# One of two pairs of weight sums taken ahead, during the up projection, and two more steps of the down projection by seven products

## The chip, the cores and the metric

The kernel runs on one core of a Trainium2 chip. The metric is the device time of one execution in microseconds; lower is better. The median before is 1215.54 us of 3 runs (1215.43 to 1217.35).

## The reference

The kernel computes one layer of a hybrid decoder for 256 tokens (and 16 prepended ones, dropped from the output) of width 2048, all in float32. What matters here is the last part, the gated feed-forward network:

```python
u = rmsnorm(h, norm_ffn)
up = causal_dwconv(u @ w_up, ffn_conv_w, ffn_conv_b)     # 2048 -> 2 x 5632
gate, val = jnp.split(up, [FFN_DIM], axis=-1)
h = h + (jax.nn.silu(gate) * val) @ w_down               # 5632 -> 2048
h = rmsnorm(h, norm_final)                               # then 16 tokens dropped
```

Ahead of it come the input projection, eight retention heads, four mLSTM heads and the output projection. They aren't touched.

## The kernel before, in words

**Products.** TensorE multiplies in a reduced format (`F32R`), so every operand is split: ScalarE casts it to a high part, VectorE subtracts to get the low part, and a product takes three matmuls (high by high, high by low, low by high). `load_w` (L122) does this for weights: an SP load into `wraw` (4 buffers), the cast into `whi` (5 buffers, L128) and the subtraction into `wlo` (5 buffers, L130).

**Up projection.** The 44 column blocks of the feed-forward width are done in two halves of 22 (`NHF`). For each, `project` (L147) runs twice, for gate and value, each over two half tiles of 512 KB: 48 matmuls with the weights stationary and 258 columns of `uh` and `ul` moving (L137 to L140). The result is scaled out of PSUM by VectorE (L626), passed through the convolution (`conv3`), the gate's SiLU and the product, and split for the down projection: into `mh`, `ml` where the step is a plain one, into `sh`, `sl` where it goes by seven products. For the latter GpSimd (POOL) also makes four sums of blocks (L735 to L738) in `x_tile(0)`. During the first half VectorE transposes `h` from `hT` into `hn` (L622), four blocks at a time from j = 2 to 17; after that `hT` holds nothing that is needed.

**Down projection.** After each half of the up projection its 22 blocks are multiplied by their rows of `w_down`: 11 steps (`NQD`), each of two blocks, for two pairs of output column blocks (b = 0 and b = 2; each block has 512 columns). A plain step takes 2 x 512 KB through `load_step`, and `product` (L747) makes four products of 6 matmuls of 512 columns, 24 in all, into the four banks `cs`. A fast step (`FAST`, six of eleven) is a 2 x 2 block product by Winograd's form with seven block products of 3 matmuls, 21 in all (`seven`, L765). Its weights come in one 1 MB load into one of two places in the dead `hT` (`left`, two turns, L773). VectorE then makes four sums of weight blocks: two at once in `ta` (L776), and one each in `tb` (L777, L778); ScalarE and VectorE split four groups of blocks (L707, L709) and TensorE multiplies (L792 to L795), partly into `cs`, partly into four banks `ps` that are shared between blocks. After the last fast step `share` (L813) combines `ps` into the residual stream `hn` by DMAs that accumulate (`onto`, L811, POOL's queue).

**The last pass** (half 1, b = 2) runs its steps in an order written out by hand, with step `BOTH` done plainly from the fast step's splits, and leaves the second column block of the last `lag` = 4 plain steps for the end (`alone`): first for row block 0, whose norm and output then run (`gather`, `finish`) while TensorE does row block 1 in two pieces of 256 columns. Ahead of that, squares and gains of finished blocks (`squares` on ScalarE, `times_gain` on POOL) are hung behind fast steps; `reached` (L801) is a one-column POOL read that sets their place.

**Order.** Each engine works through its own queue in order. The queues are ordered by the compiler's scheduler, which simulates when each instruction could start and may place work well ahead of its place in the program (the first `hT<-in_wd` load is issued at 683.83 us, some 40 us ahead of its use); `tc.issue_after` pins single instructions.

Of the kernel before, what the change touches and what calls it, by code (L numbers as in the profile page):

```python
# [10 lines left out]
F32 = mybir.dt.float32  # L11
F32R = mybir.dt.float32r
# [4 lines left out]
P = 128  # L17
# [66 lines left out]
def trunk(ctx: ExitStack, tc: tile.TileContext, io, out: bass.AP):  # L84
# [18 lines left out]
        a = _COLS[name][0]  # L103
        return par[:, a + i : a + i + n]

    ident = consts.tile([P, P], F32, name="ident")
    ones = consts.tile([P, P], F32, name="ones")
    nc.vector.memset(ones, 1.0)
    inv_dm = consts.tile([P, P], F32, name="inv_dm")
    nc.vector.memset(inv_dm, 1.0 / DM)  # L110
    inv_ret = consts.tile([P, P], F32R, name="inv_ret")
    inv_ml = consts.tile([P, P], F32R, name="inv_ml")
    epsc = consts.tile([P, 1], F32, name="epsc")
    nc.vector.memset(epsc, EPS)
    rstd1 = consts.tile([P, T], F32, name="rstd1")
    rstd2 = consts.tile([P, NQ], F32, name="rstd2")
    norms = consts.tile([P, RH + 2 * MH], F32, name="norms")


    last_load = None  # L120
# [54 lines left out]

    pa_cm = pool("pa", 1, side="right")
    pa = pa_cm.__enter__()
    xh = pa.tile([P, KT, T], F32R, name="xh")
    xl = pa.tile([P, KT, T], F32R, name="xl")
    rope = pa.tile([P, 4, T], F32, name="rope")  # L180
# [388 lines left out]
    wk2_cm = pool("wk2", 2, side="right")  # L569
    wk2 = wk2_cm.__enter__()  # L570

    ssq = up.tile([P, NQ], F32, name="ssq")
    sq2_cm = pool("sq2", 2, side="right")
    sq2 = sq2_cm.__enter__()

# [28 lines left out]
    def norm2():  # L604
        ms2 = at.tile([P, 512], F32, name="atps")
        nc.tensor.matmul(ms2[:, :NQ], inv_dm, ssq, start=True, stop=True)
        r0, rt = (midp.tile([P, 512], F32, name=f"x{i}") for i in range(2))
# [5 lines left out]
    midp = midp_cm.__enter__()  # L613
    NHF = NF // 2
    ss4 = midp.tile([P, 2, 5], F32, name="ss4")

    def transposed_h(i, a):

# [77 lines left out]
    def x_tile(i):  # L696
        return midp.tile([P, 512], F32, name=f"x{i}")

    for half in range(2):
        mh = midp.tile([P, 2 * len(PLAIN), SEQ], F32R, name="mh")  # L700
        ml = midp.tile([P, 2 * len(PLAIN), SEQ], F32R, name="ml")
        sh = midp.tile([P, len(FAST), 7, P], F32R, name="sh")
# [8 lines left out]
        for jj in range(NHF):  # L711
            j = half * NHF + jj
            pair = []
            for s in range(2):
                pair.append(project(io["wu"][2 * j + s], uh, ul, 0))
                if j == 0 and s == 0:
                    norm2()
            gt = conv3(pair[0], j, "gt")
            vt = conv3(pair[1], NF + j, "vt")
            nc.scalar.activation(gt, gt, AF.Silu)  # L720
            nc.vector.tensor_tensor(out=gt, in0=gt, in1=vt, op=ALU.mult)
            q, i = divmod(jj, 2)
            if q in PLAIN:
                k = 2 * PLAIN.index(q) + i
                copied, parted = split(mh[:, k, :], ml[:, k, :], gt)
            elif i == 0:
                f = FAST.index(q)
                even = gt
                copied, parted = split(sh[:, f, A11, :], sl[:, f, A11, :], gt[:, 0:P])
            else:  # L730
                e11, e21, e12, e22 = even[:, 0:P], even[:, P:], gt[:, 0:P], gt[:, P:]
                if half == 1 and q == BOTH:
                    split(*a21, e21)
                sums = x_tile(0).rearrange("p (a t) -> p a t", a=4)
                nc.gpsimd.tensor_tensor(out=sums[:, S1, :], in0=e21, in1=e22, op=ALU.add)  # L735
                nc.gpsimd.tensor_tensor(out=sums[:, S3, :], in0=e11, in1=e21, op=ALU.subtract)
# [28 lines left out]
        def seven(b, q, cs, ps, first, last, after, norm):  # L765
# [7 lines left out]
            nc.sync.dma_start(raw, io["wd7"][b // 2, half * NQD + q])  # L773
            ta, tb = (wpool.tile([P, 2, 512], F32, name="wraw", bufs=4) for _ in range(2))

            nc.vector.tensor_tensor(out=ta, in0=raw[:, 1:3, :], in1=raw[:, 0:1, :].to_broadcast([P, 2, 512]), op=ALU.subtract)  # L776
            nc.vector.tensor_tensor(out=tb[:, 0, :], in0=raw[:, 2, :], in1=ta[:, 0, :], op=ALU.add)  # L777
            nc.vector.tensor_tensor(out=tb[:, 1, :], in0=raw[:, 3, :], in1=tb[:, 0, :], op=ALU.subtract)  # L778
            copied = None
            for w, to in (  # L780
                (raw[:, 2:4, :], ((S4, cs[0, 1], False, False), (A12, cs[0, 0], False, False))),
                (raw[:, 1:2, :], ((A11, ps[0], first, last),)),
                (ta, ((S1, ps[3], first, last), (S3, ps[1], first, last))),
                (tb, ((S2, ps[2], first, last), (A22, cs[1, 0], False, False))),
            ):
                hi = wpool.tile([P, 2, 512], F32R, name="whi", bufs=5)
                lo = wpool.tile([P, 2, 512], F32R, name="wlo", bufs=5)
# [8 lines left out]
            if norm:  # L796

                with tc.issue_after(copied.ins):
                    for g in norm:
                        squares(*g)  # L800
                reached = nc.gpsimd.tensor_tensor(out=junk[:, 0:1], in0=tb[:, 1, 0:1], in1=tb[:, 1, 0:1], op=ALU.add)  # L801
# [8 lines left out]

            nc.gpsimd.dma_start(block(tt, b), x, accum_op=ALU.add)  # L811

        def share(ps, b):  # L813

            p1, p7, p6, p5 = ps
            x6, x7, x5, x1 = (x_tile(i) for i in range(4))
# [7 lines left out]
            nc.vector.tensor_tensor(out=x5, in0=x7, in1=p5, op=ALU.subtract)  # L824
            onto(1, b + 1, x5)

# [13 lines left out]
        def load_step(b, q, to=wpool):  # L840
            return load_w(io["wd"][b, half * NQD + q], [P, 2, 512], to)

        lag = 4
        gains = []
        emptied = None
        for b in (0, 2):
# [4 lines left out]
            ps = [mm.tile([P, 512], F32, name="mmps") for _ in range(4)]  # L851

            final = half == 1 and b == 2
            steps = [0, 1, 3, 2, 6, 4, BOTH, 5, 7, 9, 10] if final else range(NQD)
            fast = [q for q in steps if q in FAST and not (final and q == BOTH)]
            plain = [q for q in steps if q not in fast]
            alone = plain[-lag:] if final else []
            for q in steps:
                if q in fast:
# [2 lines left out]
                        due, gains = gains[:1], gains[1:]  # L862
                    seven(b, q, cs, ps, q == fast[0], q == fast[-1], emptied, due)
                    if q == fast[-1]:
                        share(ps, b)
                    continue
                for j in range(2):
                    if j == 1 and q in alone:
# [127 lines left out]
```

## Time and profile before

| | |
|---|---|
| median of 3 runs | 1215.54 us |
| the profiled execution's own time | 1215.93 us |
| its span, first to last instruction | 1214.2 us |
| TensorE / VectorE / ScalarE / POOL busy | 99% / 78% / 58% / 11% |
| up projection, first and second half | about 474 to 723 and 841 to 1090 us |
| down projection, first and second half | about 723 to 840 and 1090 to 1205 us |
| granted TensorE clock | 0.998 |
| read from HBM / written | 222.98 / 4.46 MB |

In the profile PE is TensorE's matmuls and PEld its weight loads, DVE is VectorE, ACT is ScalarE, POOL is GpSimd, SP the engine that issues most DMAs. A row of groups gives line, engine, operation, tile written and tiles read, shape, and count, then busy time in us and mean ns of one, then the engine's idle time just before these instructions and what ended most of it. A row of a timeline or of the chain of waits begins with start and duration in us. A row of DMA issues ends with KB of each and the median us from issue to landing. A busy PE isn't PE at its peak, since matmuls overlap; the distance between starts is what one costs. Idle time on an engine that doesn't set the end costs nothing.

### The profile page before, as it was taken

The numbers are of one execution on the slowest core, as the hardware profiler recorded it, in microseconds if no ns is written. First come the engines' busy times: TensorE is split into PE (matmuls) and PEld (weight loads), VectorE is DVE, ScalarE is ACT, GpSimd is POOL, SyncE is SP. The second block draws the span as 40 slices with busy tenths as digits, with TensorE's granted clock in tenths as the row PEclk, the third lists the DMA queues.
The fourth block names the chain that finished last, engine by engine and source line by source line (L and its number), as shares of the span: only waits on it lengthen the run. The fifth ranks groups of instructions, "written<-read, shape, count | busy, mean of one in ns | idle before, by whom it ended". The sixth has DMA issues, their size and how long they took to land.

```text
span 1214.2 us, 22554 instructions
## 1 busy us (share of the span) xinstructions
PE 1203.5 (99%) x8965; PEld 1156.7 (95%) x8965; DVE 950.8 (78%) x1399; ACT 704.2 (58%) x954; POOL 131.0 (11%) x143
## 2 busy tenths in 40 slices
PE   9999999999999999999999999999999999999997
PEld 9999999999999999999999998888999999998885
DVE  8877778766765767788888789896777777789896
ACT  8647746656556556555555556665555555556564
POOL 0100001111010210010101000202020101100232
PEclk9999999999999999999999999999999999999999
DMA  7764555655564655555555634959655555535946
GB/s 277 267 218 157 167 191 169 201 170 187 183 190 140 208 180 180 182 189 180 186 175 189 247 119 170 263 218 315 229 177 189 177 188 177 188 118 195 274 167 184
DMA packets 74010, 236.25 MB, mean 195 GB/s; under 512 B 13488, under 2 KB 17712, under 8 KB 70832
## 3 DMA queue, kind: packets, MB, share of 16 engines
q1 hardware_dynamic: 68640, 223.85, 55.0%
q0 software_dynamic: 4688, 10.10, 4.1%
q8 instruction: 70, 1.15, 0.4%
q10 hardware_dynamic: 576, 0.85, 0.2%
q14 instruction: 36, 0.29, 0.1%
HBM read 222.98 MB, written 4.46 MB: 187 GB/s over the span
## 4 chain that ended last, share of the span: by engine, by line
PE 96%; DVE 1%; DMA 1%; issue 0%; ACT 0%; SPq 0%; POOL 0%; DVEq 0%; ACTq 0%
PE mmps L137 25%; PE mmps L140 25%; PE mmps L138 25%; PE atps L760 3%; PE atps L761 3%; PE atps L763 3%; PE mmps L795 2%; PE mmps L793 2%; PE mmps L792 2%; PE atps L792 1%; PE atps L795 1%; PE atps L793 1%; PE atps L379 1%; DMA hn<-x 0%; DVE wlo L709 0%; PE atps L371 0%
## 5 line engine op out<-in xcount | busy, mean ns | idle before, releaser
L128 ACT CAST whi<-wraw 128x1024 fp32r<-128x1024 f32 x358 | 375.4, 1050 | 357.9 <-PE mmps L138 250.9
L130 DVE TENSOR_TENSOR wlo<-wraw,whi 128x1024 fp32r<-128x1024 f32 x358 | 441.9, 1237 | 81.3 <-ACT whi L128 74.2
L138 PE MATMUL mmps<-ul,whi 128*128 128x258 f32 x1408 | 345.8, 283 | 0.0
L137 PE MATMUL mmps<-uh,whi 128*128 128x258 f32 x1408 | 345.5, 282 | 0.0
L137 PEld LDWEIGHTS mmps<-uh,whi 128*128 128x128 f32 x1408 | 266.1, 189 | 0.1
L138 PEld LDWEIGHTS mmps<-ul,whi 128*128 128x128 f32 x1408 | 265.1, 188 | 0.1
L137 PE MATMUL mmps<-xh,whi 128*128 128x272 f32 (+2 forms) x864 | 220.1, 287 | 0.0
L138 PE MATMUL mmps<-xl,whi 128*128 128x272 f32 (+2 forms) x864 | 218.8, 286 | 0.0
L140 PE MATMUL mmps<-uh,wlo 128*128 128x258 f32 x1408 | 198.9, 284 | 0.0
L140 PEld LDWEIGHTS mmps<-uh,wlo 128*128 128x128 f32 x1408 | 182.4, 189 | 0.0
L137 PEld LDWEIGHTS mmps<-xh,whi 128*128 128x128 f32 x864 | 162.9, 189 | 0.1
L138 PEld LDWEIGHTS mmps<-xl,whi 128*128 128x128 f32 x864 | 162.5, 188 | 0.0
L140 PE MATMUL mmps<-xh,wlo 128*128 128x272 f32 (+2 forms) x864 | 127.1, 286 | 0.0
L140 PEld LDWEIGHTS mmps<-xh,wlo 128*128 128x128 f32 x864 | 114.7, 188 | 0.0
L626 DVE TENSOR_TENSOR cu<-mmps,rstd 128x258 f32<-128x258 f32 x88 | 37.5, 426 | 78.8 <-PE mmps L140 78.5
L707 ACT CAST whi<-wraw 128x1024 fp32r<-128x1024 f32 x46 | 47.7, 1052 | 37.7 <-DVE wraw L778 22.1
L760 PE MATMUL atps<-whi,mh 128*128 128x512 f32 (+1 forms) x166 | 64.0, 387 | 0.0
L761 PE MATMUL atps<-whi,ml 128*128 128x512 f32 (+1 forms) x166 | 63.8, 386 | 0.0
L138 PE MATMUL mmps<-mixl,whi 128*128 128x258 f32 x256 | 63.1, 283 | 0.0
L137 PE MATMUL mmps<-mixh,whi 128*128 128x258 f32 x256 | 62.5, 283 | 0.0
L709 DVE TENSOR_TENSOR wlo<-wraw,whi 128x1024 fp32r<-128x1024 f32 x46 | 56.5, 1244 | 5.5 <-PE mmps L795 3.0
L707 ACT CAST whi<-hT 128x1024 fp32r<-128x1024 f32 (+1 forms) x46 | 37.4, 836 | 20.6 <-PE atps L793 7.7
(267 smaller groups left out, 1620.2 us busy)
## 6 DMA issues: line engine op xcount, KB each, us to landing
wraw<-in_wu SPq DMA_DIRECT2D x176, 512.0 KB, 3.5
wraw<-in_wi SPq DMA_DIRECT2D x108, 512.0 KB, 4.0
hT<-in_wd SPq DMA_DIRECT2D x23, 1024.0 KB, 5.3
wraw<-in_wd SPq DMA_DIRECT2D x42, 512.0 KB, 5.2
wraw<-in_wo SPq DMA_DIRECT2D x32, 512.0 KB, 3.6
hn<-x POOLq DMA_DIRECT2D x28, 256.0 KB, 6.3
wraw<-in_w SPq DMA_DIRECT2D x7, 320.0 KB, 5.1
hT<-in_xT SPq DMA_DIRECT2D x7, 272.0 KB, 5.5
```

The source lines that it names most:

```text
L128: nc.scalar.copy(hi, raw)
L130: nc.vector.tensor_tensor(out=lo, in0=raw, in1=hi.bitcast(F32), op=ALU.subtract)
L137: nc.tensor.matmul(ps, hi[:, k, :], xh(kk), start=kk == first, stop=False)
L138: nc.tensor.matmul(ps, hi[:, k, :], xl(kk), start=False, stop=False)
L140: nc.tensor.matmul(ps, lo[:, k, :], xh(kk), start=False, stop=kk == last)
L626: nc.vector.tensor_tensor(out=u, in0=ps[:, :NQ], in1=rstd2, op=ALU.mult)
L707: copied = nc.scalar.copy(hi, x)
L709: return copied, nc.vector.tensor_tensor(out=lo, in0=x, in1=hi.bitcast(F32), op=ALU.subtract)
L760: nc.tensor.matmul(ps, ah[i], hi[:, i, cols], start=first and i == 0, stop=False)
L761: nc.tensor.matmul(ps, al[i], hi[:, i, cols], start=False, stop=False)
L763: nc.tensor.matmul(ps, ah[i], lo[:, i, cols], start=False, stop=last and i == 1)
L792: nc.tensor.matmul(o, sh[:, f, m, :], hi[:, i, :], start=begin, stop=False)
```

## The change

Two more steps of eleven go by seven products: `FAST` becomes eight steps in a half and b, 31 fast steps in all instead of 23 (`BOTH` is plain in the last pass). Of the four sums of weight blocks two, those of L776, are taken earlier: `Early` loads three of a step's four blocks (768 KB) from POOL's queue during the up projection, VectorE subtracts in place one `project` later, and POOL's queue stores the two differences (512 KB) into a DRAM tile `kept`. There are 16 such units in half 0 and 15 in half 1, at written-out points (`begins`); their buffers (`homes`) are three quarters of the new tile `x4` for the first twelve of half 0, then that and the two places in the dead `hT` in turn.

A fast step of the down projection now loads the kept differences (512 KB) and one block (256 KB) into one of two places in `hT` and the two other blocks (512 KB) into `wraw`, 1.25 MB instead of 1 MB in three loads instead of one. Two sums of 512 columns stay there, in `t24`, which has one place. The order of the four groups changes with it.

Besides: in the last pass `lag` is 3 and the order of the steps is new; `share` adds block (0, 3) with VectorE instead of a DMA that accumulates. Constants that the feed-forward part doesn't read move from `consts` to `pa`, the four `x` tiles become one tile `x4`, and `ssq` lies in `hn`.

```diff
-    FAST = [1, 2, 4, 5, 7, 8]
+    FAST = [1, 2, 3, 4, 6, 7, 8, 9]
-    left = hT.rearrange("p k t -> p (k t)")[:, 0:4096].rearrange("p (i a n) -> i p a n", i=2, a=4)
+    dead = hT.rearrange("p k t -> p (k t)")[:, 0:4096].rearrange("p (a n) -> p a n", a=8)
+    left = [dead[:, 0:3, :], dead[:, 3:6, :]]
+    t24 = dead[:, 6:8, :]
...
+    class Early:
+        def __init__(self, b, q, buf):
+            self.buf = buf
+            self.kept = dram.tile([P, 2, 512], F32, name=f"kept{b}_{q % NQD}", bufs=1)
+            nc.gpsimd.dma_start(buf, io["wd7"][b // 2, q][:, 0:3, :])
+        def finish(self):
+            v = self.buf[:, 1:3, :]
+            nc.vector.tensor_tensor(out=v, in0=v, in1=self.buf[:, 0:1, :].to_broadcast([P, 2, 512]), op=ALU.subtract)
+            nc.gpsimd.dma_start(self.kept, v)
     for half in range(2):
+        units = [(b, q) for b in (0, 2) for q in FAST if (half, b, q) != (1, 2, BOTH)]
+        homes = [left[0], left[1], x4[:, 1:4, :]]
+        if half == 0:
+            begins = [2 + 3 * i for i in range(12)] + [37, 38, 40, 41][: len(units) - 12]
+            homes = 12 * [homes[2]] + homes + homes
+        else:
+            begins = [2 + 39 * i // (len(units) - 1) for i in range(len(units))]
+            homes = 6 * homes
...
                 pair.append(project(io["wu"][2 * j + s], uh, ul, 0))
+                if running:
+                    running.pop().finish()
+                if 2 * jj + s in begins:
+                    n = begins.index(2 * jj + s)
+                    b, q = units[n]
+                    running.append(Early(b, half * NQD + q, homes[n]))
+                    early[b, q] = running[-1].kept
...
-            raw = left[turn]
+            raw0 = wpool.tile([P, 2, 512], F32, name="wraw", bufs=4)
+            raw1 = left[turn]
             turn = 1 - turn
-            nc.sync.dma_start(raw, io["wd7"][b // 2, half * NQD + q])
-            ta, tb = (wpool.tile([P, 2, 512], F32, name="wraw", bufs=4) for _ in range(2))
-            nc.vector.tensor_tensor(out=ta, in0=raw[:, 1:3, :], in1=raw[:, 0:1, :].to_broadcast([P, 2, 512]), op=ALU.subtract)
-            nc.vector.tensor_tensor(out=tb[:, 0, :], in0=raw[:, 2, :], in1=ta[:, 0, :], op=ALU.add)
-            nc.vector.tensor_tensor(out=tb[:, 1, :], in0=raw[:, 3, :], in1=tb[:, 0, :], op=ALU.subtract)
+            nc.sync.dma_start(raw1[:, 1:3, :], early[b, q])
+            nc.sync.dma_start(raw1[:, 0, :], io["wd"][b + 1, half * NQD + q][:, 1, :])
+            nc.sync.dma_start(raw0, io["wd"][b, half * NQD + q])
+            nc.vector.tensor_tensor(out=t24[:, 0, :], in0=raw1[:, 0, :], in1=raw1[:, 1, :], op=ALU.add)
+            nc.vector.tensor_tensor(out=t24[:, 1, :], in0=raw0[:, 1, :], in1=t24[:, 0, :], op=ALU.subtract)
...
-            onto(0, b + 1, x6)
+            if final:
+                nc.vector.tensor_tensor(out=block(0, b + 1), in0=block(0, b + 1), in1=x6, op=ALU.add)
+            else:
+                onto(0, b + 1, x6)
...
-        lag = 4
+        lag = 3
...
-            steps = [0, 1, 3, 2, 6, 4, BOTH, 5, 7, 9, 10] if final else range(NQD)
+            steps = [0, 1, 2, 3, 5, 4, 6, 7, 8, BOTH, 10] if final else range(NQD)
```

More of the change, by code (lines that the diff above doesn't have):

```diff
@@ L570, in trunk @@
     wk2 = wk2_cm.__enter__()
-    ssq = up.tile([P, NQ], F32, name="ssq")
+    ssq = hn[:, 0, 0:NQ]
     sq2_cm = pool("sq2", 2, side="right")
@@ L606, in norm2 @@
         nc.tensor.matmul(ms2[:, :NQ], inv_dm, ssq, start=True, stop=True)
-        r0, rt = (midp.tile([P, 512], F32, name=f"x{i}") for i in range(2))
+        r0, rt = x_tile(0), x_tile(1)
         r = rsqrt_m2(r0, rt, ms2[:, :NQ], NQ, squared)
@@ L615, in trunk, with x_tile @@
     ss4 = midp.tile([P, 2, 5], F32, name="ss4")
+    x4 = midp.tile([P, 4, 512], F32, name="x4")
+    def x_tile(i):
+        return x4[:, i, :]
     def transposed_h(i, a):
@@ L800, in seven @@
                         squares(*g)
-                reached = nc.gpsimd.tensor_tensor(out=junk[:, 0:1], in0=tb[:, 1, 0:1], in1=tb[:, 1, 0:1], op=ALU.add)
+                reached = nc.gpsimd.tensor_tensor(out=junk[:, 0:1], in0=t24[:, 1, 0:1], in1=t24[:, 1, 0:1], op=ALU.add)
                 with tc.issue_after(reached.ins):
@@ L811, in onto, with share @@
             nc.gpsimd.dma_start(block(tt, b), x, accum_op=ALU.add)
-        def share(ps, b):
+        def share(ps, b, final):
             p1, p7, p6, p5 = ps
@@ L864, in trunk @@
                     if q == fast[-1]:
-                        share(ps, b)
+                        share(ps, b, final)
                     continue
```

25 lines of the change are left out of this document (12 added, 13 removed).

## The prediction

> **What bounds the kernel now.** I read the page's head and its chain first, then the timeline and chain of single stages, then the busy times by stage, then the groups by line and the DMA issues.
>
> ```profile
> span 1214.2 us, 22554 instructions
> ...
> PE 96%; DVE 1%; DMA 1%; issue 0%; ACT 0%; SPq 0%; POOL 0%; DVEq 0%; ACTq 0%
> ```
>
> The chain is TensorE nearly throughout. The chain in order of time shows how dense that is:
>
> ```profile
> 477.25 0.97 PE mmps L140 x8
> 483.02 0.97 PE mmps L140 x8
> 776.23 1.86 PE atps L763 x8
> 1145.08 1.86 PE atps L763 x8
> ```
>
> Up projection: 48 matmuls of 258 columns lie between the first two rows, 5.77 us, 0.120 us each; the eight inside a row take 0.97, also 0.12. So nothing lies between groups. Down projection: eight matmuls of 512 columns take 1.86 us, 0.2325 each. The stages:
>
> ```profile
> core 0: us, PE busy (x) PEld busy (x) DVE busy (x) ACT busy (x) POOL busy (x), PEclk, DMA share, GB/s
> 474.00:723.00 249.00, 249.00 (x2062) 248.54 (x2062) 207.10 (x307) 134.34 (x180) 22.91 (x24) 1.00 0.55 182
> 726.00:838.00 112.00, 112.00 (x493) 90.61 (x492) 97.79 (x103) 67.24 (x76) 12.60 (x15) 1.00 0.72 235
> 845.00:1090.00 245.00, 245.00 (x2037) 244.91 (x2036) 185.10 (x272) 133.46 (x179) 23.13 (x25) 1.00 0.56 181
> 1096.00:1150.00 54.00, 54.00 (x233) 43.46 (x232) 47.85 (x51) 32.88 (x38) 6.98 (x8) 1.00 0.72 229
> ```
>
> TensorE is full in both up halves (first, third row) and both downs, at full granted clock, with 0.232 us a matmul (54/233) over the whole fourth row, the same as inside a group. So a matmul removed there is time removed, as long as VectorE (DVE), 87% busy in the down (97.79/112) and 83% in the first up (207.10/249), and the DMAs keep their lead.
>
> **The change, part by part.**
>
> *Fewer matmuls.* A plain step is 4 products of 6 matmuls, 24; a step by seven products is 21. Fast steps go from 23 to 31 (8 x 2 x 2 less the last BOTH), so 8 x 3 = 24 matmuls of 512 columns go, 24 x 0.2325 = 5.6 us. (The last `alone` steps, three instead of four, only move work about within this count.)
>
> *VectorE in the down.*
>
> ```profile
> L130 DVE TENSOR_TENSOR wlo<-wraw,whi 128x1024 fp32r<-128x1024 f32 x358 | 441.9, 1237 | 81.3 <-ACT whi L128 74.2 <-PE atps L795 2.8
> L709 DVE TENSOR_TENSOR wlo<-wraw,whi 128x1024 fp32r<-128x1024 f32 x46 | 56.5, 1244 | 5.5 <-PE mmps L795 3.0 <-ACT whi L707 1.3 <-PE mmps L793 1.0
> L709 DVE TENSOR_TENSOR wlo<-hT,whi 128x1024 fp32r<-128x1024 f32 (+1 forms) x46 | 42.7, 950 | 5.5 <-ACT whi L707 5.5
> L776 DVE TENSOR_TENSOR wraw<-hT 128x1024 f32<-128x1024 f32 x23 | 29.1, 1265 | 0.1
> L777 DVE TENSOR_TENSOR wraw<-hT,wraw 128x512 f32<-128x512 f32 x23 | 16.8, 731 | 0.1
> L778 DVE TENSOR_TENSOR wraw<-hT,wraw 128x512 f32<-128x512 f32 x23 | 15.7, 683 | 0.1
> ```
>
> Splits of a fast step: 2 x 1.244 + 2 x 0.950 = 4.39 us; sums 1.265 + 0.731 + 0.683 = 2.68 before, 1.41 after, since L776 moves. Over the first down: 16 x (4.39 + 1.41) - 12 x (4.39 + 2.68) = +8.0, and 8 plain splits fewer, -9.9: -1.9 us in all. VectorE then has 95.9 us in 109.2, 88%, as now. Inside a fast step it has 5.80 us against 21 x 0.2325 = 4.88 of TensorE, so a run of four loses 3.7 us of lead; now a run of two loses 2 x (7.07 - 4.88) = 4.4 and TensorE doesn't stop. The four-run is no worse. ScalarE's casts keep their count per step.
>
> *The moved sum.* L776's 1.265 us goes into the up projection, 16 times in half 0 and 15 in half 1, with a load (768 KB) and a store (512 KB) each, from POOL's queue. Two more fast steps a half also add splits there:
>
> ```profile
> L709 DVE TENSOR_TENSOR sl<-gt,sh 128x128 fp32r<-128x128 f32 (+1 forms) x24 | 14.8, 619 | 0.0
> L709 DVE TENSOR_TENSOR sl<-x,sh 128x512 fp32r<-128x512 f32 x12 | 8.2, 686 | 0.0
> L709 DVE TENSOR_TENSOR ml<-gt,mh 128x256 fp32r<-128x256 f32 x20 | 8.4, 418 | 0.0
> ACT whi L128 <- PE mmps L138: 250.9, 200, 4.2
> ...
> L644 POOL TENSOR_TENSOR hn<-hn,gfin 128x512 f32<-128x512 f32 (+1 forms) x7 | 10.0, 1434 | 5.5 <-ACT junk L640 5.5
> ```
>
> A fast step's splits are 2 x 0.619 + 0.686 = 1.92 against 2 x 0.418, so +1.09 each. Half 0: 207.1 + 16 x 1.265 + 2.2 = 229.5 of 249, 92%; half 1: 185.1 x 249/245 + 15 x 1.265 + 2.2 = 209.3, 84%. What hides it is VectorE's idle time, 19.5 and 40 us, and the lead: the fourth row shows ScalarE waiting for TensorE to free one of five `whi`, so about four half tiles (24 x 0.120 = 2.9 us each) are ready ahead, 11.5 us, some 9 less cast and split. Without this cover each sum costs its 1.27 us, 39 us in all. I cost it at nothing.
>
> *Queued behind.* `finish` makes VectorE wait in order for POOL's load; behind it stand the weight splits and the evictions (L626), and TensorE waits for both. The store makes POOL wait for VectorE, with the four sums of L735 to L738 behind it, which ScalarE's split waits for. In the last pass `t24` has one place where `ta` and `tb` had a ring, so the next step's sums wait for POOL's read of it (L801); one whole step, 4.88 us, lies between, and I cost it at nothing, at most one times-gain on POOL, 1.4 us (L644), if late. The stored sums are read a stage later, so their landing hides behind the rest of the up projection. The constants moved to `pa` and `ssq` laid into `hn` (its reader is done in step 0, the transposes begin in step 2) add no instruction and cost nothing.
>
> *DMA.*
>
> ```profile
> wraw<-in_wu SPq DMA_DIRECT2D x176, 512.0 KB, 3.5
> hT<-in_wd SPq DMA_DIRECT2D x23, 1024.0 KB, 5.3
> wraw<-in_wd SPq DMA_DIRECT2D x42, 512.0 KB, 5.2
> hn<-x POOLq DMA_DIRECT2D x28, 256.0 KB, 6.3
> e<-in_decay POOLq DMA_DIRECT2D x8, 209.0 KB, 3.1
> gfin<-in_gfin POOLq DMA_DIRECT2D x1, 1024.0 KB, 5.4
> SPq L773 <- DVE wlo L709: 99.6, 16, 16.8
> ```
>
> First up: 16 x 1.31 MB in 249 us, 84 GB/s on top of 182, so the engines go from 55% to about 80%. A weight load lands in 3.5 us and has four `wraw` buffers, 11.5 us; even twice as long is hidden. Down: 0.26 MB more per fast step, at 1.31 MB per 4.88 us 269 GB/s, against 235 at a share of 0.72 now, so 0.82. That fits; the price is 0, up to rival B. The early load of 768 KB is nearest to 1024 KB on the same queue, 5.4 us, and lies above 209 KB, 3.1: 4.7 by interpolation; with the weights beside it I take 5. `finish` stands one project (5.77 us) later. Both ends for its wait: 0 and 3 us (accumulates, 6.3, take 3 over their 256 KB's 3.2 on that line).
>
> [...]
>
> ```profile
> L735 POOL TENSOR_TENSOR x<-gt 128x128 f32<-128x128 f32 x12 | 5.5, 461 | 119.7 <-DVE gt L721 119.7
> L736 POOL TENSOR_TENSOR x<-gt 128x128 f32<-128x128 f32 x12 | 18.0, 1502 | 253.6 <-ACT whi L128 183.7 <-PE mmps L140 36.1 <-DVE gt L721 33.8
> ```
>
> The same shape takes POOL 0.46 us in one line and 1.50 in the next: it is held by something, up to 1.04 us. [...]
>
> *The tail.*
>
> ```profile
> 1193.83 0.68 DVE L824 TENSOR_TENSOR x<-x,mmps 128x512 f32<-128x512 f32 x1
> 1200.78 0.69 DVE L829 TENSOR_TENSOR hn<-atps,hn 128x512 f32<-128x512 f32 x1 [1.65 <-DMA hn<-x]
> 1204.17 1.39 DVE L669 TENSOR_SCALAR hn<-hn,frt 128x256 f32<-128x256 f32 x2
> 1205.48 0.74 DVE L667 SCALAR_TENSOR_TENSOR hn<-hn,frt,gfin 128x512 f32<-128x512 f32 x1
> 1206.21 0.41 DVE L829 TENSOR_TENSOR hn<-atps,hn 128x256 f32<-128x256 f32 x1
> 1203.57 0.28 PE L760 MATMUL atps<-whi,mh 128*128 128x256 f32 x1
> 1204.76 0.40 PE L763 MATMUL atps<-wlo,mh 128*128 128x256 f32 x2
> ```
>
> TensorE ends at 1205.1; the last add starts at 1206.21 only because row 0's scaling (L669, L667) stands before it. Ten 256-column matmuls lie between the last two rows, 0.119 us each, so with three `alone` steps the cover for row 0's finish is 36 x 0.119 = 4.3 us, not 5.7, and the stretch from the last seven products to the end is 24 + 18 matmuls of 0.2325 and those 4.3, 14.1 us instead of 16.9. The accumulate of block (0, 3), for which L829 waits 1.65 us, becomes a VectorE add of 0.68. That of block (1, 3) stays: its source L824 ends 10.6 us before TensorE now, 10.6 - 2.8 = 7.8 after, and an accumulate takes 6.3 (`hn<-x`, above) and its issue. Gain up to 1 us, loss up to 1.5; I take 0.
>
> Sum against the profiled run's own 1215.93 us: -5.6, 1210.3. That run lies 0.39 above the median of 1215.54, so in medians 1210.0.
>
> **The rivals.**
>
> *A, slower: VectorE waits for the early loads.* Against it: project and load have about the same length, and the lead is large. For it: half 0 has 19.5 us idle and 9 of lead for 16 waits, so it decides from (19.5 + 9) / 16 = 1.8 us each; at the upper end, 3, TensorE loses 48 - 28.5 = 19.5 us: 1229.5. Half 1 (49 us for 45) loses nothing. [...]
>
> *B: the two `left` places starve the runs of four.* SP already waits 99.6 us for such a place (the row above). A place is held some 4 us (sums and splits until its third group) and refilled in 5.3 to 7: two steps take up to 11, 5.5 each against 4.88, so 2.5 us a run, eight runs, 20 us; the 4 to 5 us of lead that five `wlo` give (one fast step) should take most of it. A third through: 1217.
>
> *C: the tail is longer.* Block (1, 3)'s accumulate lands after TensorE's end, or the finish of row 0, with 1.4 us less cover, moves the last add: +2.5, 1212.5.
>
> *D: the tail is shorter* by the 1 us in which the last add stood behind row 0: 1209.
>
> **How the numbers follow.** A measurement of this kernel tells some 0.2% (2.4 us) from no change, so faster means under 1213.1. Forecast 0.57, D 0.10, C 0.10, B 0.13, A 0.10. Faster takes the forecast, D, most of C and a quarter of B: 0.77; same the rest of C and a quarter of B, 0.09; slower half of B and A, rounded, 0.14. The range goes from 1208.0 (D and its spread) to 1219.0, which leaves out A and a little of B.
>
> **What would show it.** Right: up halves still at 5.77 us a project, down matmuls at 0.232 us, 945 matmuls of 512 columns instead of 963, VectorE at 92% and 84% in the ups. Wrong: rows "DVE <- DMA" for the new subtraction over 28 us in half 0 (A); TensorE idle behind L793 or L795 with "DMA hT<-" before it in steps 2 to 4 or 7 to 9 (B); over 9.1 us from TensorE's end to the span's (C).

## The result, and the profile after

The changed kernel takes 1234.4 us (median of 5 runs, 1233.81 to 1235.89); the kernel before, timed beside it, takes 1216.29 us (1215.43 to 1217.35). The ratio is 1.0151, with a 95% interval from 1.0137 to 1.0165: slower by 18.1 us, where 5.6 us less were forecast.

The profiled execution took 1234.4 us. First the head of its page and its chain:

```profile
span 1232.6 us, 22858 instructions
...
PE 83%; DMA 7%; DVE 5%; issue 3%; ACT 2%; POOL 0%; DVEq 0%; ACTq 0%; POOLq 0%; SPq 0%
```

TensorE held 96% of the chain; now it holds 83%, and DMA and VectorE come in. The busy times by stage, over the windows that the prediction used and one in the last pass (columns as there):

```profile
474.00:723.00 249.00, 249.00 (x2055) 248.41 (x2054) 213.51 (x315) 130.59 (x183) 45.74 (x64) 1.00 0.77 268
726.00:838.00 112.00, 107.58 (x451) 84.81 (x450) 98.29 (x113) 67.39 (x79) 10.62 (x14) 0.98 0.79 247
845.00:1090.00 245.00, 242.67 (x2007) 241.84 (x2006) 195.34 (x278) 131.23 (x182) 50.13 (x61) 1.00 0.79 271
1096.00:1150.00 54.00, 52.97 (x232) 42.44 (x231) 45.26 (x53) 34.20 (x39) 1.48 (x2) 1.00 0.65 217
1150.00:1215.00 65.00, 57.40 (x233) 42.38 (x232) 55.42 (x58) 36.60 (x48) 17.87 (x17) 1.00 0.72 208
```

The first up projection is full, with 16 early sums in it. The first down has 4.4 us without a matmul, the second up 2.3, the last two windows, in the second down, 1.0 and 7.6. VectorE is busy 98.29 us in the first down, as before (97.79): its share doesn't show what happened.

For every run below I give what TensorE lost by stage: the time from each matmul's start to the next one's, less 0.2325 us (512 columns) or 0.120 (258), summed, and less what a stage without a stall gives (some matmul records are missing): 0.4 us in a down, 0.6 in an up of the kernel before and 1.2 in an up of all the others. In those the matmuls of 258 columns start 0.1206 us apart instead of 0.1203, all through the up and without a gap; no run shows why. It makes the changed kernel's ups 1.1 us longer together, and its first up starts 1.2 us earlier, so the two cancel. "Tail" is the time from the last matmul's start to the end of the span.

| | up 0 | down 0 | up 1 | down 1 | tail |
|---|---|---|---|---|---|
| before | 0 | 0 | 0 | 0 | 9.3 |
| after | 0 | 7.1 | 3.4 | 12.4 | 10.6 |

22.9 lost, 1.3 more tail and 5.6 saved make 18.6; the span grew by 18.4. The waits that grew, from the list of waits of the changed kernel (us in total, times, longest):

```profile
ACT whi L736 <- DVE hT L815: 32.7, 18, 3.4
DVE x L714 <- DMA x<-in_wd: 18.7, 13, 4.9
ACT x L919 <- DMA hn<-x: 14.8, 9, 2.4
PE atps L796 <- ACT x L919: 5.4, 5, 1.8
PE mmps L829 <- ACT whi L736: 4.7, 6, 1.1
DVE hT L815 <- POOL junk L838: 3.3, 1, 3.3
```

ScalarE's casts (L736) wait for the second sum of `t24` (L815) on VectorE, and TensorE (L829) waits for such casts. The end copies (L919) wait for accumulates that still read their tiles, and TensorE (L796) waits for the copies' banks. The early subtraction (L714) waits 18.7 us for its loads in `x4`, all in half 0, where TensorE lost nothing.

Where the first one comes from stands in VectorE's timeline at the end of the first run of four (start, duration, line; idle time before it in brackets):

```profile
757.05 1.23 DVE L738 TENSOR_TENSOR wlo<-hT,whi 128x1024 fp32r<-128x1024 f32 x1 [0.59 <-ACT whi L736]
758.20 1.22 DVE L738 TENSOR_TENSOR wlo<-wraw,whi 128x1024 fp32r<-128x1024 f32 x1
759.33 0.69 DVE L814 TENSOR_TENSOR hT<-hT 128x512 f32<-128x512 f32 x1
759.93 1.82 DVE L738 TENSOR_TENSOR wlo<-hT,whi 128x1024 fp32r<-128x1024 f32 x2
761.67 0.68 DVE L815 TENSOR_TENSOR hT<-wraw,hT 128x512 f32<-128x512 f32 x1
763.55 1.23 DVE L738 TENSOR_TENSOR wlo<-hT,whi 128x1024 fp32r<-128x1024 f32 x1 [1.19 <-ACT whi L736]
...
770.01 1.23 DVE L738 TENSOR_TENSOR wlo<-hT,whi 128x1024 fp32r<-128x1024 f32 x1 [1.17 <-ACT whi L736]
```

A fast step takes VectorE 6.50 us here (757.05 to 763.55, and 6.46 to 770.01): 5.30 of work and 1.2 of waiting. The second sum L815 stands last, behind the splits of `raw1`. ScalarE's cast of `t24` can start only behind it, takes 1.05 us, and VectorE's split of `t24` waits for that cast. `t24` has one place, so the next step's L814 comes only behind this split; and ScalarE, in order, casts the next `raw0` only behind the cast of `t24`. So VectorE has nothing else to do. (In the first of the two steps TensorE frees the cast's place in `whi` in the same 0.1 us in which the sum ends, and ScalarE's row names TensorE; in the second it names the sum.) TensorE needs 4.88 us for the step. In the kernel before, the sums of the next step stand among the splits of this one, and VectorE doesn't wait between them:

```profile
752.53 1.21 DVE L776 TENSOR_TENSOR wraw<-hT 128x1024 f32<-128x1024 f32 x1
753.66 0.68 DVE L709 TENSOR_TENSOR wlo<-hT,whi 128x512 fp32r<-128x512 f32 x1
754.26 0.68 DVE L778 TENSOR_TENSOR wraw<-hT,wraw 128x512 f32<-128x512 f32 x1
754.87 1.21 DVE L709 TENSOR_TENSOR wlo<-wraw,whi 128x1024 fp32r<-128x1024 f32 x1
756.00 0.68 DVE L777 TENSOR_TENSOR wraw<-hT,wraw 128x512 f32<-128x512 f32 x1
756.61 1.21 DVE L709 TENSOR_TENSOR wlo<-wraw,whi 128x1024 fp32r<-128x1024 f32 x1
757.74 0.68 DVE L778 TENSOR_TENSOR wraw<-hT,wraw 128x512 f32<-128x512 f32 x1
```

What follows the run is shown by ScalarE's timeline, from the first plain step behind it:

```profile
776.19 1.05 ACT L121 CAST whi<-wraw 128x1024 fp32r<-128x1024 f32 x1 [3.36 <-DMA wraw<-in_wd]
...
785.29 0.59 ACT L919 COPY x<-atps 128x512 f32<-128x512 f32 x1 [2.13 <-DMA hn<-x]
787.91 0.59 ACT L919 COPY x<-atps 128x512 f32<-128x512 f32 x1 [2.03 <-DMA hn<-x]
```

The plain step's weights are late, `share`'s sums stand behind their splits in VectorE's order, so its accumulates land late, and the end copies, which reuse those tiles after one plain step (two before), wait for them.

### The profile page after: what moved, and what is told of

Its sections match the earlier page's. It is cut to its first block, busy times and chain, and to the rows that moved or that the text cites. A ratio compares the mean times of both kernels' runs of the same rounds, so it can differ in the third digit from the quotient of the medians.

```text
span 1232.6 us, 22858 instructions
## 1 busy us (share of the span) xinstructions
PE 1205.7 (98%) x8935; PEld 1152.3 (93%) x8935; DVE 978.9 (79%) x1444; ACT 707.0 (57%) x974; POOL 176.2 (14%) x220
## 4 chain that ended last, share of the span: by engine, by line
PE 83%; DMA 7%; DVE 5%; issue 3%; ACT 2%; POOL 0%; DVEq 0%; ACTq 0%; POOLq 0%; SPq 0%
PE mmps L130 23%; PE mmps L133 23%; PE mmps L131 23%; DMA hn<-x 3%; DMA wraw<-in_wu 2%; PE mmps L829 1%; PE mmps L830 1%; PE mmps L832 1%; DMA wraw<-in_wd 1%; DVE wlo L123 1%; PE atps L829 1%; PE atps L830 1%; PE atps L832 1%; PE atps L796 1%; PE atps L799 1%
## 5 line engine op out<-in xcount | busy, mean ns | idle before, releaser
L121 ACT CAST whi<-wraw 128x1024 fp32r<-128x1024 f32 x342 | 353.8, 1047 | 224.2 <-PE mmps L131 167.7
L123 DVE TENSOR_TENSOR wlo<-wraw,whi 128x1024 fp32r<-128x1024 f32 x342 | 420.9, 1234 | 63.6 <-ACT whi L121 61.9
L736 ACT CAST whi<-hT 128x1024 fp32r<-128x1024 f32 (+1 forms) x93 | 81.4, 904 | 61.1 <-DVE hT L815 32.7
L738 DVE TENSOR_TENSOR wlo<-hT,whi 128x1024 fp32r<-128x1024 f32 (+1 forms) x93 | 93.9, 1041 | 15.6 <-ACT whi L736 15.0
L829 PE MATMUL mmps<-whi,sh 128*128 128x512 f32 x124 | 49.8, 401 | 4.9 <-ACT whi L736 4.7
L756 ACT ACTIVATE gt<-gt 128x256 f32<-128x256 f32 x44 | 18.3, 417 | 55.5 <-DVE gt L635 55.2
L830 PE MATMUL mmps<-whi,sl 128*128 128x512 f32 x124 | 49.0, 395 | 0.0
```

Of the source, the lines that this page charges most:

```text
L121: nc.scalar.copy(hi, raw)
L123: nc.vector.tensor_tensor(out=lo, in0=raw, in1=hi.bitcast(F32), op=ALU.subtract)
L736: copied = nc.scalar.copy(hi, x)
L738: return copied, nc.vector.tensor_tensor(out=lo, in0=x, in1=hi.bitcast(F32), op=ALU.subtract)
L829: nc.tensor.matmul(o, sh[:, f, m, :], hi[:, i, :], start=begin, stop=False)
L830: nc.tensor.matmul(o, sl[:, f, m, :], hi[:, i, :], start=False, stop=False)
```

## The experiments

The first four expectations number their theories among themselves; from the fifth on, theory 1 is VectorE's amount of work, 2 the late loads, 3 the norm's chain, 4 the bunched early units, 5 the round trip just shown. Losses of all runs, as above:

| run | us | up 0 | down 0 | up 1 | down 1 | tail |
|---|---|---|---|---|---|---|
| e1_own_half1 | 1233.91 | 0.5 | 8.4 | 3.4 | 9.9 | 10.7 |
| e2_run_of_8 | 1250.95 | 0 | 16.7 | 6.8 | 14.3 | 11.0 |
| e3_early_only | 1226.17 | 0 | 2.1 | 5.7 | 2.0 | 9.1 |
| e4_fast8_no_early | 1237.73 | 0 | 8.8 | 0.1 | 17.4 | 10.0 |
| e5_no_sums | 1225.40 | 6.8 | 1.7 | 0 | 4.0 | 11.3 |
| e6_room | 1235.13 | 3.4 | 6.5 | 2.7 | 10.3 | 11.2 |
| e7_norm | 1230.61 | 0 | 5.9 | 4.0 | 9.1 | 10.4 |
| e8_pinned | 1236.86 | 0 | 12.5 | 0 | 12.1 | 11.0 |
| e9_sum_first | 1224.30 | 0 | 2.3 | 4.3 | 6.0 | 10.2 |
| e10_all | 1216.25 | 0 | 1.1 | 0 | 1.8 | 12.0 |
| e11_seven | 1216.33 | 0 | 1.0 | 0 | 0 | 11.2 |
| e12_all_add | 1216.37 | 0 | 1.2 | 0 | 1.9 | 10.4 |
| e13_seven_add | 1215.79 | 0 | 1.0 | 0 | 0 | 10.4 |

The last two times are medians of 12 and 11 runs, the others one run each; a single run of the kernel before beside e1 to e4 took 1217.7 us, beside e5 to e8 1215.97, beside e9 to e11 1220.43, so single times are good to some 5 us at worst, and the losses by stage carry the argument. They have noise too: half 0's down, which e1, e6 and e7 leave as it is, lost 8.4, 6.5 and 5.9 us there against 7.1, so a difference of 1 to 2 us in a stage of a single run says little.

**e1: end copies of half 1 in a tile of their own.**

```diff
+            y4 = more.tile([P, 4, 512], F32, name="y4", bufs=1)
...
-                        x = x_tile(2 * j + n)
+                        x = y4[:, 2 * j + n, :] if half == 1 else x_tile(2 * j + n)
```

> The changed kernel, but in half 1 the four copies at the end of pass b = 0 go to tiles of their own instead of the x tiles, out of which share's accumulates are still being read. Theory 1 (the end copies wait for share's accumulates, because one plain step lies between instead of two): in half 1 the rows 'ACT x L919 <- DMA hn<-x' vanish, TensorE's 3.1 us lost between 1150 and 1160 us of the span fall under 1, and some of the 6.7 us lost later in the last pass goes with it; half 0 keeps its 7.2 us. Time 1229 to 1231. Rival 2 (VectorE runs out of lead in the runs of four fast steps, and the copies only show it): the loss moves to another wait, 1233 to 1235.

The time stays. Half 1's down loses 9.9 us instead of 12.4, less from 1140 to 1160 us (1.4 against 4.4) and a little more behind it. So the end copies are a place where the loss shows, with at most some 2.5 us of their own.

**e2: eight fast steps in one run, two plain steps behind it.**

```diff
-    FAST = [1, 2, 3, 4, 6, 7, 8, 9]
+    FAST = [1, 2, 3, 4, 5, 6, 7, 8]
...
-            steps = [0, 1, 2, 3, 5, 4, 6, 7, 8, BOTH, 10] if final else range(NQD)
+            steps = [0, 1, 2, 3, BOTH, 4, 5, 6, 7, 9, 10] if final else range(NQD)
```

> The changed kernel with the fast steps 1 to 8 and the plain ones 0, 9 and 10: as many matmuls, but again two plain steps (11.2 us) between the last fast step and the end of a pass, and one run of eight fast steps instead of two of four. Theory 1: the waits of the end copies for accumulates vanish in both halves, about 10 us of the 23 us lost: 1224. Rival 2: a run of eight loses 8 x (5.8 - 4.88) = 7.4 us of VectorE's lead against the 4.9 it has, so 2.5 us or more are lost at the end of each of four passes instead of 1.2 now: if it is the main cause, 1234 or more.

The same matmuls and sums, and 16.5 us more: the length of the runs is what costs, and two plain steps at the end don't make up for it.

**e3: the early sums alone,** with the six fast steps, the order, the lag and the accumulate of block (0, 3) of before.

```diff
-    FAST = [1, 2, 3, 4, 6, 7, 8, 9]
+    FAST = [1, 2, 4, 5, 7, 8]
...
-        lag = 3
+        lag = 4
...
-            steps = [0, 1, 2, 3, 5, 4, 6, 7, 8, BOTH, 10] if final else range(NQD)
+            steps = [0, 1, 3, 2, 6, 4, BOTH, 5, 7, 9, 10] if final else range(NQD)
```

> The six fast steps, the order of the last pass and lag 4 of the kernel before, with the sums taken early and kept in DRAM (23 of them) and the new loads in the down. Theory 1 and rival 2: nothing is lost in the down, so 1215 to 1217, within 2 us of before. Rival 3 (the early loads and subtractions cost TensorE time in the up projection): TensorE loses 2 us or more in the ups, most in half 1 where the changed kernel lost 3.4: 1218 to 1222.

With no matmul fewer the early sums, and the new form of the fast steps that comes with them, cost some 10 us: 5.7 in half 1's up, where VectorE waits for a load once for 3.57 us, and 4.1 in the downs. The tail is 9.1, as before: its growth belongs to `lag`, or to what comes with it.

**e4: eight fast steps without early sums,** all four sums in the down, from one load of four blocks with the groups ordered as before; of the edit only the groups are shown.

```diff
-                (raw0, ((A11, ps[0], first, last), (A12, cs[0, 0], False, False))),
...
+                (ta, ((S1, ps[3], first, last), (S3, ps[1], first, last))),
+                (tb, ((S2, ps[2], first, last), (A22, cs[1, 0], False, False))),
```

> The eight fast steps, the order and the x4 tile of the changed kernel, but nothing taken early: all four sums in the down, from one 1 MB load, as before. Theory 1: the end copies still wait, some 10 us lost as in the changed kernel. Rival 2: VectorE has 7.07 us of work for 4.88 of a fast step, a run of four loses 8.8 us against 4.9 of lead, so some 3 to 4 us more are lost in each of eight runs: 1245 to 1260. If theory 1 alone, 1230 to 1235. Rival 3: the ups are free of loss.

The ups lose nothing, the downs 26.2 us. The first down by engine:

```profile
726.00:838.00 112.00, 105.56 (x447) 83.02 (x446) 109.14 (x120) 65.52 (x76) 7.95 (x9) 1.00 0.66 212
```

VectorE is busy 109.14 of 112 us: here it is the bound. With early sums it has 98.29 and the down still loses 7.1, so there something else than its amount of work counts as well.

**e5: the sums of `t24` left out.**

```diff
-            nc.vector.tensor_tensor(out=t24[:, 0, :], in0=raw1[:, 0, :], in1=raw1[:, 1, :], op=ALU.add)
-            nc.vector.tensor_tensor(out=t24[:, 1, :], in0=raw0[:, 1, :], in1=t24[:, 0, :], op=ALU.subtract)
```

> Leaves out the two sums of t24 (VectorE, 1.41 us a fast step); its weight is stale data, every load, cast, split and matmul stays. Theory 1, VectorE's own work uses up its lead in a run of four: a fast step then costs VectorE 4.4 us against TensorE's 4.88, and the downs lose under 6 us instead of 22: 1216 to 1219 us. Theory 2, the weights land late because raw0 takes places in the ring of the plain steps: every load and place stays, so the loss stays, 1230 us or more.

The kernel then multiplies with what lies in `t24`; everything else stays. The downs lose 5.7 us instead of 19.5, as theory 1 expected, with every load in place. But the run takes away two things at once: 1.4 us of VectorE's work, and the wait of ScalarE's cast for the sum. It can't tell them apart. TensorE also met a stall that it didn't have in the changed kernel, in half 0's up: behind an early load that landed in 8.1 us, where the median of this run is 7.4.

```profile
622.35 1.23 DVE L714 TENSOR_TENSOR x<-x 128x1024 f32<-128x1024 f32 x1 [4.89 <-DMA x<-in_wd]
```

VectorE stood 4.89 us in order behind that load, and TensorE lost 6.8: rival A's mechanism, in one of 16 places (e6 met it too, 3.46 us and 3.4 lost). The length of the wait doesn't decide alone: the changed kernel has one of 4.89 us too, at 591.90, and e13 one of 5.34, and neither lost anything. In e5 it was the third of some 5 us within 56 us (566.77, 594.58, 622.35), so the lead was probably used up already; that is argued, not shown.

**e6: room in half 1's down.** `raw0` gets two places of its own instead of one in the ring of the plain steps, `t24` two.

```diff
-            raw0 = wpool.tile([P, 2, 512], F32, name="wraw", bufs=4)
+            raw0 = more.tile([P, 2, 512], F32, name="raw0", bufs=2) if half == 1 else wpool.tile([P, 2, 512], F32, name="wraw", bufs=4)
...
+            t24 = t24b if half == 1 and turn else t24a
```

> Half 1's down alone gets room: raw0 has two places of its own instead of one in the ring of four, and t24 has two places. Half 0's down is as in the changed kernel. Theory 2 (late loads for want of places): half 1's down loses 5 us or less instead of 12.6, half 0's still 9: 1227 us. Theory 1 (VectorE's work): nothing of VectorE's work goes, half 1 loses 10 or more: 1232 to 1235 us.

Half 1's down loses 10.3 instead of 12.4, but not in the same places. The first 4.7 us are the edit's own, at 1097 to 1120 us, where the changed kernel loses nothing: `raw0`'s new places lie in a pool that opens only when the up projection is done, so the first load is issued at 1102.9 us instead of some 20 us earlier, and VectorE waits 3.0 us for it, TensorE 2.8. From there to 1170 us it loses 4.5 (the changed kernel 5.6), with one end copy waiting 8.2 us for an accumulate, and behind that 1.5 (the changed kernel 7.1). In half 1's down VectorE's splits wait 2.1 us for casts, two times, where it was 11.6 and ten: with two places for `t24` the round trip is gone for the most part. So the room is worth more than the time says, some 6 to 7 us. How much of it comes from `raw0`'s places (theory 2), from `t24`'s or from POOL's read of `t24` (theory 3) this run can't tell.

**e7: the norm off the path.** The first squares come a fast step later, and `reached` reads `raw0`, so that the next sums into `t24` don't wait for POOL.

```diff
-                    if final and q != fast[0]:
+                    if final and q not in fast[:2]:
...
-                reached = nc.gpsimd.tensor_tensor(out=junk[:, 0:1], in0=t24[:, 1, 0:1], in1=t24[:, 1, 0:1], op=ALU.add)
+                reached = nc.gpsimd.tensor_tensor(out=junk[:, 0:1], in0=raw0[:, 0, 0:1], in1=raw0[:, 0, 0:1], op=ALU.add)
```

> In the last pass the first sum of squares comes one fast step later, and POOL's reached reads raw0 instead of t24, so that the next sums into t24 no longer wait for POOL. Theory 3, the norm's chain (accumulate, squares on ScalarE, reached on POOL, t24 on VectorE) stalls the last pass: 4 to 5 us go from 1150 to 1200 us of the span, 1229 to 1230 us. Theory 1 (VectorE's work): the loss moves to the next step, 1232 to 1235 us.

3.8 us less, 3.3 of them in half 1's down, where VectorE's wait for POOL was 3.3: theory 3 has its share, a little less than it expected.

**e8: each early subtraction held behind the split of the step before.**

```diff
                 if running:
-                    running.pop().finish()
+                    with tc.issue_after(parted.ins):
+                        running.pop().finish()
```

> Each early subtraction is held behind VectorE's last split of the up-projection step before it, so that the units come spread as written and not in bunches. Theory 4, the bunches disturb: the loss of 2.0 us in half 1's up and of 1.5 us at the end of half 0's down goes, and the accumulates land sooner there: 1229 to 1231 us. If bunching is harmless: 1233 to 1236 us.

Half 1's up loses nothing now: there theory 4 holds. But half 0's last units come so late that the first down's steps wait for what they keep (VectorE once 3.1 us, ScalarE once 3.5 us, for the load of it), and down 0 loses 5.4 more. Spreading helps where units have time, in half 1.

**e9: the second sum in front of the splits.** Only the order on VectorE changes.

```diff
-            nc.vector.tensor_tensor(out=t24[:, 1, :], in0=raw0[:, 1, :], in1=t24[:, 0, :], op=ALU.subtract)
+            summed = nc.vector.tensor_tensor(out=t24[:, 1, :], in0=raw0[:, 1, :], in1=t24[:, 0, :], op=ALU.subtract)
...
-                    copied, _ = split(hi[:, :n, :], lo[:, :n, :], w)
+                    copied, _ = split(hi[:, :n, :], lo[:, :n, :], w, None if w is raw0 else summed)
```

> Only VectorE's order changes: the splits of raw1 and of t24 are held behind the second sum (L815), so that ScalarE's cast of t24, in order on its engine, finds it ready. Theory 5, the loss of the runs of four is a round trip (late sum on VectorE, cast on ScalarE, split on VectorE, 1.8 us of idle VectorE in each fast step of 6.5 us): VectorE's period falls from 6.5 to about 5.8 us and the downs lose 10 us or less instead of 22: 1220 to 1225 us. Theory 1 (VectorE's amount of work alone): no instruction goes, so the time stays within 3 us of 1234.

10.1 us less, without one instruction less. VectorE's timeline of the same stretch:

```profile
757.13 1.22 DVE L738 TENSOR_TENSOR wlo<-wraw,whi 128x1024 fp32r<-128x1024 f32 x1
758.27 0.68 DVE L814 TENSOR_TENSOR hT<-hT 128x512 f32<-128x512 f32 x1
758.99 0.69 DVE L815 TENSOR_TENSOR hT<-wraw,hT 128x512 f32<-128x512 f32 x1
759.60 2.96 DVE L738 TENSOR_TENSOR wlo<-hT,whi 128x1024 fp32r<-128x1024 f32 x3
762.47 1.22 DVE L738 TENSOR_TENSOR wlo<-wraw,whi 128x1024 fp32r<-128x1024 f32 x1
```

A fast step is 5.34 us (757.13 to 762.47, the next one the same), with no idle time in it; it was 6.50. Theory 5 is shown, and theory 1, VectorE's amount of work alone, falls as the cause of most of the loss: at this amount of work a run of four falls behind TensorE by 4 x (5.34 - 4.88) = 1.8 us, with the round trip by 4 x (6.50 - 4.88) = 6.5. The downs lose 8.3 us instead of 19.5. (The sum also frees `raw0` earlier for the next load, so some of this gain can be theory 2's; the 1.2 us in each step weren't a wait for a load.)

**e10: the sum first, and e1, e7 and e8 (in half 1 alone) with it.**

```diff
+                    with tc.issue_after(parted.ins) if half == 1 else nullcontext():
```

> The sum first as in the run before, and the three edits tried singly: end copies of half 1 in a tile of their own, the norm one step later with reached reading raw0, and half 1's early subtractions held to their steps. If the causes are separate, their gains add: some 4 us for the norm and 3 for the units on top of the sum's gain, 1214 to 1219 us. If they feed one shortage of lead, most of it is the sum's: within 2 us of that run.

Another 8.05 us. Singly, on the changed kernel, e1 and e7 took 0.7 and 3.9 us off what TensorE lost, and e8 in half 1 alone 3.7 (up 1 and down 1), 8.3 together; here the loss falls by 9.7 from e9's. So the gains about add, as separate causes would. TensorE now loses 2.9 us in all, but the tail has grown to 12.0. VectorE's timeline there:

```profile
1202.31 0.69 DVE L871 TENSOR_TENSOR hn<-atps,hn 128x512 f32<-128x512 f32 x1 [2.91 <-DMA hn<-x]
```

The last adds wait for the accumulate of block (1, 3), as rival C had it.

**e11: e10 with seven fast steps.**

```diff
-    FAST = [1, 2, 3, 4, 6, 7, 8, 9]
+    FAST = [1, 2, 3, 5, 6, 8, 9]
...
-            steps = [0, 1, 2, 3, 5, 4, 6, 7, 8, BOTH, 10] if final else range(NQD)
+            steps = [0, 1, 2, 4, 3, 5, 7, 6, 8, BOTH, 10] if final else range(NQD)
```

> All four edits, and seven fast steps instead of eight (runs of three, two and two, four plain steps): 12 matmuls of 512 columns more than with eight, 2.8 us each half pair, 957 in all. Theory 1 with 5: in runs of three and two VectorE's 5.8 us a fast step is made up by the plain steps, the downs lose under 3 us and the kernel takes 1213 to 1217 us. If the early units or the late loads cost by themselves, as in the run with six fast steps: 1220 us or more.

TensorE loses 1.0 us in all, 1.9 less than with eight, for 12 matmuls (2.8 us) more, and its tail is 0.8 shorter. Same time.

**e12: e10, with the last accumulate as an add on VectorE.**

```diff
+            if final:
+                nc.vector.tensor_tensor(out=block(1, b + 1), in0=block(1, b + 1), in1=x5, op=ALU.add)
+            else:
+                onto(1, b + 1, x5)
```

> The run with all four edits, with its tail mended: in the last pass VectorE adds the share of block (1, 3) itself (0.69 us) instead of handing it to an accumulate, for which the last adds waited 2.91 us there. Rival C of the prediction (the accumulate of block (1, 3) lands after TensorE's end) then gives back 2 to 2.8 us: the tail falls from 12.0 to 9.2 to 10 us, the kernel takes 1213 to 1214.5 us and is faster than the kernel before by some 2 us. If the tail is held by row 0's finish instead, it stays at 1216.

The wait is gone and the tail falls to 10.4; the profiled execution took 1214.35 us. But the median of 12 runs is 1216.37 us (1214.35 to 1220.6) against 1215.91 for the kernel before: ratio 1.0004, interval 0.9992 to 1.0015. The forecast gain isn't there, and executions differ by 6 us; those of the kernel before by 1.4, but for one of 16 at 1220.99.

**e13: e11 with that add.**

```diff
-    FAST = [1, 2, 3, 4, 6, 7, 8, 9]
+    FAST = [1, 2, 3, 5, 6, 8, 9]
...
+                nc.vector.tensor_tensor(out=block(1, b + 1), in0=block(1, b + 1), in1=x5, op=ALU.add)
```

> Seven fast steps instead of eight, with all five edits. The run with eight spread over 6 us from execution to execution. Theory 5 with a thin lead: in runs of four VectorE has only some 0.5 us of slack a step, so late loads reach TensorE in some executions; with runs of three and two between four plain steps they don't: executions within 1.5 us of each other as the kernel before has them, median 1213.5 to 1215 us, 1 to 2.5 us faster than the kernel before. If the spread comes from something else (the up projection with 80% busy DMA engines), it stays at 4 to 6 us and the median at 1216.

The spread falls to 2.7 us (1214.5 to 1217.19; the kernel before beside it, 1215.21 to 1218.81). That fits runs of four with a thin lead, but 12 and 11 runs on two chips don't show it. The median is 1215.79 us against 1215.83: ratio 0.9997, interval 0.9988 to 1.0007. Of 2.8 us of matmuls saved, 1.0 goes into the stall behind the first down's first pass and 1.1 into the tail, 10.4 against 9.3. No version beat the kernel before by what can be measured.

## Why the prediction was wrong, step by step

*Fewer matmuls*: right. 945 matmuls of 512 columns and 36 of 256 are in the trace. In e12's profiled execution the last matmul starts 2.8 us earlier than in the kernel before, with 3.1 us lost: together 5.9 against the 5.6 worked out.

*VectorE in the down*: this is the step that failed, in its sentences "Inside a fast step it has 5.80 us" and "The four-run is no worse". Two errors lie in it. The sum of row means is neither the work nor the time: the work is 5.34 us, since each instruction starts some 0.08 us before the one ahead of it ends, and the time was 6.50, because the change put a round trip VectorE, ScalarE, VectorE into each step. Before, `ta` and `tb` came from a ring, and the sums for the next step stood among the splits of this one; now `t24` has one place, and its second sum came last. The prediction did ask what the single place costs, and answered it for POOL's read in the last pass alone. And a plain step, in which VectorE has 2.5 us of splits for 5.6 of TensorE, comes after two fast steps in the kernel before and only after four now. e9 shows the round trip, e2 that the length of the runs costs; e5 and e6 agree, but change two things at once. Of the 24 us that the forecast missed, e9's order gives back 10, with e10's edits 18.

*The moved sum*: half right. Half 0's 16 sums cost nothing in this execution (in e5 6.8 us, in e6 3.4), though the early loads took 6.8 and 7.7 us where 5 were taken. VectorE waited 19.9 us for them in half 0, under the 28 that were to show rival A, and was busy 86% and 80% in the ups (213.51 of 249, 195.34 of 245), not 92% and 84%: the forecast added durations that overlap, and half 0's window now holds less of the down's work done ahead (3.8 us of it instead of 8.3). The DMA rows:

```profile
x<-in_wd POOLq DMA_DIRECT2D x18, 768.0 KB, 6.8
hT<-in_wd POOLq DMA_DIRECT2D x13, 768.0 KB, 7.7
hn<-x POOLq DMA_DIRECT2D x27, 256.0 KB, 7.1
```

Half 1 "loses nothing", I wrote under rival A, and it lost 3.4 us with twice the idle time. The units of half 1 didn't come where `begins` puts them: they ran as soon as their places came free, in bunches, with loads issued from 824 to 954 us, the first among half 0's last accumulates. Held to their steps (e8, e10) they cost half 1's up nothing.

*Queued behind*: "I cost it at nothing" was wrong for `t24`. From the last pass, on VectorE:

```profile
1175.70 1.75 DVE L815 TENSOR_TENSOR hT<-wraw,hT 128x512 f32<-128x512 f32 x1 [3.25 <-POOL junk L838]
...
1181.38 1.78 DVE L814 TENSOR_TENSOR hT<-hT 128x512 f32<-128x512 f32 x1
```

POOL's `reached` waits for ScalarE's squares, these for an accumulate, and VectorE's next sum into the one `t24` for `reached`. I had priced POOL's own instruction and not what it waits for. e7: 3.8 us.

*DMA* and rival B: TensorE didn't wait for `hT<-` loads in steps 2 to 4, and in e9, with the same two `left` places, a fast step takes 5.34 us without a wait for a load. Rival B is out; e6 leaves these places as they are and says nothing of it. The late loads of the plain step behind a run remain as one link among several, whose own price stays open.

*The tail*: rival C was right, 10.6 us from the last matmul against 9.3. Its two causes are both there: with the accumulate gone the tail falls from 12.0 to 10.4 (e10, e12), with `lag` and the order of before it is 9.1 (e3). That the shorter cover of row 0's finish makes the rest is argued, not shown alone.

*The range* left out any stall of the downs except rival B. The 88% of VectorE over the whole down, "as now", was read as cover. It was right as a share (98.29 of 112) and said nothing of the run of four, in which VectorE has to be counted by itself.

## What to carry to other kernels

Count a step on an engine from the start of one such step to the next, waits included, and look for the chain through the other engines that closes it: where a ring of places becomes a single one, sum, cast and split of neighbouring steps can no longer overlap, and the order in which they are issued decides (6.50 us a step here, 5.34 with the sum first). Average busy shares don't price a pattern that changes from short to long runs; add up the lead through the longest run instead. And a load or sum that is to come at a set time has to be held there: here the scheduler took the loads of half 1 as soon as their places were free, from 824 to 954 us.

## What the runs showed of the hardware

Behind two stalls TensorE's granted clock fell. The changed kernel's busy times around the end of its first pass:

```profile
786.00:788.30 2.30, 2.30 (x6) 1.82 (x7) 0.00 (x0) 0.39 (x1) 0.87 (x1) 0.50 1.11 265
```

The granted clock is 0.50 there, and matmuls of 512 columns start 0.43 us apart instead of 0.2325, after 3.4 us (782.52 to 785.93) in which TensorE was busy for 1.25. The six matmuls from 785.93 to 788.66 take 2.73 us instead of 1.40, so 1.3 us went there on top of the stall. In e5 the same followed 3.7 us (621.50 to 625.20) in which TensorE was busy for 0.77: over the next 6.3 us the granted clock was 0.52, with matmuls of 258 columns 0.215 us apart instead of 0.120. From these numbers I estimate some 6.0 us at half speed there, 2.6 us more. A single pause of 1.93 us between two starts in the changed kernel (1159.84 to 1161.77) left the clock as it was: 1.00 from 1161.77 to 1164.80. What sets the clock these three cases don't show.

In the last pass, L814 took 1.78 us (1181.38) instead of its median of 0.68 and L815 1.75 (1175.70) while POOL's gain of 1.3 to 2.3 us (L649) ran beside them. Both ended 0.55 us after the gain did, at 1183.16 and 1177.45 against 1182.62 and 1176.90. What held them no run shows, nor whether it is what held the prediction's row on POOL (1.50 us against 0.46).
